# Gate rows moved from the head of the last projection into the stick-breaking stage, and the last reciprocal root moved from GpSimd to ScalarE

## The chip, the cores and the metric

The kernel runs on one core of a Trainium2 chip. That core has four engines that compute: TensorE (PE, its weight loads are listed apart as PEld), VectorE (DVE), ScalarE (ACT) and GpSimd (POOL). SyncE (SP) issues most of the transfers. Each engine works through its own queue in order and waits on semaphores for the others. The metric is the device time of one execution in microseconds (us), as the median of three runs.

## What is computed

Two layers of a streaming encoder on a sequence of 512 tokens, each of 1024 values in fp32, and a last RMS norm. The first layer has a pooling mixer and a spatial gate, the second a gated linear attention (GLA) and a stick-breaking attention of 8 heads. Each layer ends in an output projection of 2048 inputs on 1024 outputs, multiplied by a gate row and added to the residual stream. The reference, cut to what the change touches:

```python
def ada_modulate(x, c, norm_g, ada_w, ada_b):
    ada = jax.nn.silu(c) @ ada_w + ada_b
    shift, scale, gate = jnp.split(ada, 3, axis=-1)
    h = rmsnorm(x, norm_g) * (1.0 + scale[:, None, :]) + shift[:, None, :]
    return h, gate[:, None, :]
...
def odd_layer(x, c, norm_g, ada_w, ada_b, in_w, gate_w, gate_b, gla_norm_g, out_w):
    h, gate_res = ada_modulate(x, c, norm_g, ada_w, ada_b)
...
    y = jnp.concatenate([yc, yd], axis=-1) * jax.nn.silu(gate)
    return x + gate_res * (y @ out_w)
...
def rmsnorm(x, g):
    y = xf * lax.rsqrt(jnp.mean(xf * xf, axis=-1, keepdims=True) + EPS)
    return (y * g.astype(jnp.float32)).astype(x.dtype)
```

## The kernel before

**Matrix products.** Every fp32 operand is split into a high part of type fp32r and the remainder, also fp32r. ACT copies the high part (L183 for weights, L188 for activations), DVE subtracts (L184, L189), and TensorE runs three matmuls for each product (L197, L198, L199). One weight tile is 128x1024 fp32 (512 KB): SP loads it into one of 4 `raw` buffers (L166), and its split takes one of 3 `whi`/`wlo` pairs. One tile serves 24 matmuls of 128x512.

**Order.** A scheduler of the framework orders DVE, ACT, POOL and SP by readiness and program order. For the GLA and stick-breaking stages TensorE's order is written by hand: `boundary()` counts gaps of 12 matmuls, `at(g, f)` hangs a function on gap `g`, and `g0` is the first gap of the stick-breaking stage. Each head (`add_head`) adds score matmuls (L776), transposes (L803) and output matmuls (L811) between the projections' matmuls. The last two steps of GLA's second pair (`norm`, matmuls L719 and L720) still lie in the gaps behind `g0`. That stage ends at `order.close()`. PSUM has 6 banks with the tag `mm` for projections and 2 with the tag `aux` for everything else.

**Gate rows.** `gate_rows(1)` (L320, called at L878) makes the second layer's gate as rows that all partitions hold: eight times DVE multiplies a 128x128 tile of ones by one gate column (`rep`, L327), TensorE transposes it (L328), and for each four ACT copies the PSUM bank to `gbc` (L329). `rep` has 4 buffers (tag `diag`). The code stands behind the stick-breaking stage, and TensorE's order there is the scheduler's.

**Last projection.** `out_proj` (called at L896) runs outputs 0 to 511 for all four blocks of 128 tokens, 8 weight tiles of 24 matmuls; then outputs 512 to 1023 for blocks 0 and 1, and for blocks 2 and 3, 8 tiles of 12 matmuls each. After each block's last matmul DVE multiplies by `gbc` (L344) and adds to `x` (L345), and ACT squares with a sum over the row (L334). `scale_first` (L893) multiplies the first half of `x` by the norm's weights `fg`. `final` (L882) adds the two sums on DVE (`ssum`, L359), makes the reciprocal root on POOL in two 128x1 steps (L292, L293), scales the halves on ACT (L886) and DVE (L887), and sends them out through ACT's and SP's queues (L890).

Of the kernel before, what the change touches and what calls it, by code (L numbers as in the profile page):

```python
# [15 lines left out]
D = 1024  # L16
# [80 lines left out]
def trunk(ctx: ExitStack, tc: tile.TileContext, d, out):  # L97
# [8 lines left out]
    def nm(s):  # L106
        uid[0] += 1
        return f"{s}_{uid[0]}"
# [10 lines left out]
    def bank(tag="mm"):  # L119
        return psum.tile([P, 512], F32, name=nm(tag), tag=tag, bufs=MM_BUFS if tag == "mm" else 8 - MM_BUFS)  # L120
# [43 lines left out]
    def raw(src, w=1024):  # L164
        t = pool.tile([P, 1024], F32, name=nm("raw"), tag="raw", bufs=BUFS["raw"])
        nc.sync.dma_start(out=t[:, :w], in_=src)  # L166
        return t
# [12 lines left out]
    def split_w(t, w=1024):  # L180
        hi = pool.tile([P, 1024], F32R, name=nm("whi"), tag="whi", bufs=BUFS["w"])
        lo = pool.tile([P, 1024], F32R, name=nm("wlo"), tag="wlo", bufs=BUFS["w"])
        A.activation(out=hi[:, :w], in_=t[:, :w], func=AF.Copy)  # L183
        V.tensor_tensor(out=lo[:, :w], in0=t[:, :w], in1=hi.bitcast(F32)[:, :w], op=ALU.subtract)  # L184
        return hi, lo
# [21 lines left out]
    def stream(src, ahead=0):  # L207

        n, ready = [0], []

        def nxt():
            while len(ready) <= ahead and n[0] < src.shape[0]:
                ready.append(split_w(raw(src[n[0]])))
                n[0] += 1
            return ready.pop(0)

        def deepen(k):
            nonlocal ahead
            ahead = k
        nxt.deepen = deepen  # L220
        return nxt

    def c_unit(nxt, evac, between=lambda: None, quarter=lambda: None):
# [77 lines left out]
    def modulate(l, k, tbs, xn):  # L301
# [15 lines left out]
            V.tensor_copy(out=h_hi[k][:, r], in_=h[:, :w])  # L317
        V.tensor_tensor(out=h_lo[k][:, r], in0=h[:, :w], in1=h_hi[k].bitcast(F32)[:, r], op=ALU.subtract)  # L318

    def gate_rows(l):  # L320
        g = big("gbc")
        for n in range(2):
            ps = bank("aux")
            for i in range(4):
                c = 24 * l + 16 + 4 * n + i
                t = pool.tile([P, P], F32, name=nm("rep"), tag="diag", bufs=4)
                V.tensor_scalar(out=t, in0=ones, scalar1=ada[:, c:c + 1], scalar2=None, op0=ALU.mult)  # L327
                T.transpose(ps[:, i * P:(i + 1) * P], t, ident)  # L328
            A.copy(out=g[:, n * 512:(n + 1) * 512], in_=ps)  # L329
        return g  # L330


    def square(src, c):
        A.activation(out=junk, in_=src, func=AF.Square, accum_out=ss[:, c:c + 1])  # L334

    def out_proj(wo, y, gbc, ssc, after, mid=lambda: None):

        kept = {}

        def evac(n):  # L340
            def f(t, ps):
                c = slice(n * 512, (n + 1) * 512)
                u = slot("misc")
                V.tensor_tensor(out=u, in0=ps, in1=gbc[:, c], op=ALU.mult)  # L344
                V.tensor_tensor(out=x[t][:, c], in0=x[t][:, c], in1=u, op=ALU.add)  # L345
                square(x[t][:, c], ssc + 2 * t + n)
            return f
        t_unit(lambda kp: split_w(raw(wo[kp])), 8, y_left(y, range(TB), kept), evac(0))
        mid()
        late = lambda: None  # L350
        for tbs in ((0, 1), (2, 3)):
            t_unit(lambda kp: split_w(raw(wo[8 + kp])), 8, y_left(y, tbs, kept), evac(1), tbs,
                   ((tbs, (0, 1, 2)), late, (tbs, (3, 4)), (tbs[:1], (5, 6, 7)), (tbs[1:], (5, 6, 7))))
            late = after(tbs)
        return late
# [182 lines left out]

    def preload():
        pre.append(tc.keep_in_program_order(A.preload_act_table_set("natural_log_exp_and_others")))  # L540
    late = out_proj(d["wo0"], [y[i] for i in Y_ORDER[0]], gbc, 16, ln1, preload)


    nxt = stream(d["w1"])
# [63 lines left out]
    def at(g, f):  # L608
        steps.setdefault(g, []).append(f)
# [218 lines left out]
    def add_head(hd, g):  # L828
        block, wt = {}, {}
        at(g + 12, lambda: last.append(stick_out(hd, wt)))  # L830
        for i in range(3):
            at(g + i, lambda i=i: stick_weights(q[hd], k[hd], i, block))
            at(g + 9 + i, lambda i=i: stick_turn(block, TURNS[i], wt))
    g0 = gap[0]
    for c in range(4):
        add_head(2 * c, g0 + 12 * c + 8)
        add_head(2 * c + 1, g0 + 12 * c + 14)
# [14 lines left out]
    for c in range(4, 8):  # L852
# [7 lines left out]
        def evac(j, ps, sg=sg):  # L860
            held.append((sg, j, ps))
# [13 lines left out]
            held.clear()  # L875
    order.close()

    gbc = gate_rows(1)  # L878
    fg = big("fg")
    nc.sync.dma_start(out=fg, in_=d["fg"].to_broadcast([P, D]))  # L880

    def final(tbs):  # L882
        for t in tbs:
            r = token_rstd(t, 24)
            V.tensor_tensor(out=x[t][:, 512:], in0=x[t][:, 512:], in1=fg[:, 512:], op=ALU.mult)
            A.mul(out=x[t][:, :512], in_=x[t][:, :512], mul=r)  # L886
            V.tensor_scalar(out=x[t][:, 512:], in0=x[t][:, 512:], scalar1=r, scalar2=None, op0=ALU.mult)  # L887
            for n, e in ((1, nc.sync), (0, nc.scalar)):
                c = slice(n * 512, (n + 1) * 512)
                e.dma_start(out=out[t * P:(t + 1) * P, c], in_=x[t][:, c])  # L890
        return lambda: None

    def scale_first():  # L893
        for t in range(TB):
            V.tensor_tensor(out=x[t][:, :512], in0=x[t][:, :512], in1=fg[:, :512], op=ALU.mult)
    out_proj(d["wo1"], [y[i] for i in Y_ORDER[1]], gbc, 24, final, scale_first)  # L896


BUFS = {"big": 5, "y": 16, "kq": 8, "z": 6, "sp": 3, "r": 7, "misc": 3, "silu": 2, "raw": 4, "w": 3}
# [16 lines left out]
```

## Time and profile before

| | |
|---|---|
| Time, median of 3 runs | 843.73 us (843.17 to 845.31) |
| Profiled execution: time | 840.86 us |
| Profiled execution: span, first to last instruction | 839.0 us |
| PE busy | 817.4 us, 97% of the span |
| DVE, ACT, POOL busy | 61%, 47%, 7% |
| Mean granted TensorE clock | 0.997 |

The profile is of one execution. Starts are in microseconds from the span's first instruction. Matmuls are pipelined, so one that is listed with 0.39 us is followed by the next after some 0.23 us; what TensorE gets done is read from the starts. An idle time stands in brackets with the engine and line that ended it. Line numbers are those of the kernel before.

### The profile page before, as it was taken

The numbers are of one execution on the slowest core, as the hardware profiler recorded it, in microseconds if no ns is written. First come the engines' busy times: TensorE is split into PE (matmuls) and PEld (weight loads), VectorE is DVE, ScalarE is ACT, GpSimd is POOL, SyncE is SP. The second block draws the span as 40 slices with busy tenths as digits, with TensorE's granted clock in tenths as the row PEclk, the third lists the DMA queues.
The fourth block names the chain that finished last, engine by engine and source line by source line (L and its number), as shares of the span: only waits on it lengthen the run. The fifth ranks groups of instructions, "written<-read, shape, count | busy, mean of one in ns | idle before, by whom it ended". The sixth has DMA issues, their size and how long they took to land.

```text
span 839.0 us, 9962 instructions
## 1 busy us (share of the span) xinstructions
PE 817.4 (97%) x3688; PEld 660.5 (79%) x3688; DVE 512.2 (61%) x805; ACT 396.7 (47%) x663; POOL 61.0 (7%) x131
## 2 busy tenths in 40 slices
PE   5999999999999999999999999999999999989996
PEld 3878888888888887777878888877777777768884
DVE  6866664688684377743564543475757677433875
ACT  5463221233243356554353423575757678443553
POOL 3001111100000000000000000011010101020011
PEclk9999999999999999999999999999999999999998
DMA  8886555555562335412322221222221212222362
GB/s 285 307 290 208 189 157 195 182 169 166 187 200 79 101 126 177 161 67 100 101 76 65 78 84 51 93 84 75 76 76 53 88 39 98 78 98 97 113 206 87
DMA packets 31362, 108.31 MB, mean 129 GB/s; under 512 B 3633, under 2 KB 3761, under 8 KB 31314
## 3 DMA queue, kind: packets, MB, share of 16 engines
q1 hardware_dynamic: 30738, 106.63, 38.0%
q10 hardware_dynamic: 576, 1.05, 0.3%
q8 instruction: 29, 0.48, 0.2%
q14 instruction: 19, 0.16, 0.1%
HBM read 105.56 MB, written 2.10 MB: 128 GB/s over the span
## 4 chain that ended last, share of the span: by engine, by line
PE 89%; DVE 4%; DMA 3%; ACT 1%; issue 1%; POOL 1%; SPq 0%; POOLq 0%; ACTq 0%; DVEq 0%
PE mm L198 26%; PE mm L199 26%; PE mm L197 25%; PE aux L776 2%; PE aux L811 2%; DVE wlo L184 1%; DMA raw<-in_wfirst 1%; PE aux L803 1%; DVE raw L173 1%; DMA raw<-in_w 1%; PE aux L463 1%; PE aux L687 1%; DMA x<-in_x 1%; ACT whi L183 1%; PE aux L689 1%
## 5 line engine op out<-in xcount | busy, mean ns | idle before, releaser
L184 DVE TENSOR_TENSOR wlo<-raw,whi 128x1024 fp32r<-128x1024 f32 (+1 forms) x146 | 177.5, 1218 | 123.6 <-ACT whi L183 123.5
L183 ACT ACTIVATE whi<-raw 128x1024 fp32r<-128x1024 f32 (+1 forms) x146 | 152.5, 1044 | 197.7 <-PE mm L198 82.3
L197 PE MATMUL mm<-hhi,whi 128*128 128x512 f32 x576 | 233.3, 405 | 0.0
L199 PE MATMUL mm<-hhi,wlo 128*128 128x512 f32 x576 | 225.0, 391 | 0.0
L198 PE MATMUL mm<-hlo,whi 128*128 128x512 f32 x576 | 224.5, 390 | 0.0
L197 PEld LDWEIGHTS mm<-hhi,whi 128*128 128x128 f32 x576 | 108.2, 188 | 23.6 <-issue 2.7
L198 PEld LDWEIGHTS mm<-hlo,whi 128*128 128x128 f32 x576 | 108.3, 188 | 23.1 <-issue 1.9
L199 PEld LDWEIGHTS mm<-hhi,wlo 128*128 128x128 f32 x576 | 108.1, 188 | 23.3
L173 DVE CUSTOM_DVE_ANT_0 raw<-raw,sc,cols 128x1024 f32<-128x1024 f32 x48 | 61.5, 1283 | 53.7 <-DMA raw<-in_adaT 53.5
L197 PE MATMUL mm<-whi,hhi 128*128 128x512 f32 x192 | 78.2, 410 | 0.2 <-DVE hhi L317 0.2
L198 PE MATMUL mm<-wlo,hhi 128*128 128x512 f32 x192 | 76.2, 397 | 0.1
L199 PE MATMUL mm<-whi,hlo 128*128 128x512 f32 x192 | 74.6, 396 | 0.1
L199 PE MATMUL mm<-whi,r 128*128 128x512 f32 x160 | 62.6, 391 | 0.0
L197 PE MATMUL mm<-whi,r 128*128 128x512 f32 x160 | 62.4, 391 | 0.0
L198 PE MATMUL mm<-wlo,r 128*128 128x512 f32 x160 | 62.4, 390 | 0.0
L197 PEld LDWEIGHTS mm<-whi,hhi 128*128 128x128 f32 x192 | 36.4, 191 | 10.2 <-issue 2.1
L199 PEld LDWEIGHTS mm<-whi,hlo 128*128 128x128 f32 x192 | 36.5, 190 | 8.8 <-DVE hlo L318 1.0
L198 PEld LDWEIGHTS mm<-wlo,hhi 128*128 128x128 f32 x192 | 36.7, 191 | 7.5 <-DVE wlo L184 0.5
L188 ACT ACTIVATE r<-y 128x256 fp32r<-128x256 f32 (+1 forms) x60 | 27.0, 479 | 29.2 <-PE mm L199 23.2
L189 DVE TENSOR_TENSOR r<-y,r 128x256 fp32r<-128x256 f32 (+1 forms) x60 | 29.1, 509 | 19.1 <-PE mm L198 16.1
L198 PEld LDWEIGHTS mm<-wlo,r 128*128 128x128 f32 x160 | 30.0, 188 | 6.4 <-DVE wlo L184 0.3
L197 PEld LDWEIGHTS mm<-whi,r 128*128 128x128 f32 x160 | 30.0, 188 | 6.2
(185 smaller groups left out, 1028.3 us busy)
## 6 DMA issues: line engine op xcount, KB each, us to landing
raw<-in_w SPq DMA_DIRECT2D x90, 512.0 KB, 3.3
raw<-in_adaT SPq DMA_DIRECT2D x48, 512.0 KB, 4.0
raw<-in_wo SPq DMA_DIRECT2D x48, 512.0 KB, 3.3
raw<-in_wfirst SPq DMA_DIRECT2D x8, 384.0 KB, 4.4
x<-in_x SPq DMA_DIRECT2D x4, 512.0 KB, 5.2
kq<-in_poolw SPq DMA_DIRECT2D x4, 256.0 KB, 5.3
out<-x SPq DMA_DIRECT2D x4, 256.0 KB, 2.1
out<-x ACTq DMA_DIRECT2D x4, 256.0 KB, 2.6
```

What stands on the lines that cost most here:

```text
L173: V.tensor_tensor_reduce(out=t, in0=t, in1=sc, scale=1.0, scalar=cols[:, C_AB[l] + b:C_AB[l] + b + 1], op0=ALU.mult, op1=ALU.add, accum_ou ...
L183: A.activation(out=hi[:, :w], in_=t[:, :w], func=AF.Copy)
L184: V.tensor_tensor(out=lo[:, :w], in0=t[:, :w], in1=hi.bitcast(F32)[:, :w], op=ALU.subtract)
L188: A.activation(out=hi, in_=src, func=AF.Copy)
L189: V.tensor_tensor(out=lo, in0=src, in1=hi.bitcast(F32), op=ALU.subtract)
L197: T.matmul(o, lh, rh, start=start, stop=False)
L198: T.matmul(o, lh, rl, start=False, stop=False)
L199: T.matmul(o, ll, rh, start=False, stop=stop)
L463: T.matmul(ps[:, t * P:(t + 1) * P], v[t][:, hd * P:(hd + 1) * P], sguw[hd // 4][:, c], start=True, stop=True)
L687: T.matmul(ov, gv[c][p][:, c0:c0 + P], att[p][:, j * P:(j + 1) * P], start=True, stop=p == 0)
L776: T.matmul(ps[:, c0:c0 + (t + 1) * P], q[:, t * P:(t + 1) * P], k[:, :(t + 1) * P], start=True, stop=True)
L811: T.matmul(ps[:, s * P:], sv[hd // 4][s][:, hd % 4 * P:(hd % 4 + 1) * P], wt[s], start=s == 0, stop=s == 3)
```

## The change

`gate_rows` is cut into `gate_half`, which returns the transposes and the copy as a second step. Both halves of the second layer's gate are hung on gaps `g0 + 2` to `g0 + 5` of the hand-written order. The stream of the last projection's weights is made before the stage, and its first load and split stand at gap `g0 + 60` (`prime`). `final` no longer uses POOL: DVE prepares mean of the first half plus epsilon (`first_sum`, L905 of the changed kernel), and ACT takes `Ln` with the second half's sum and then `Exp` of minus one half of it. A load of the activation table that has both is written ahead of `scale_first`.

```diff
+        def prime():
+            ready.append(split_w(raw(src[n[0]])))
+            n[0] += 1
+        nxt.prime = prime
...
+    def gate_half(l, n):
+        reps = []
+        for i in range(4):
+            c = 24 * l + 16 + 4 * n + i
+            reps.append(pool.tile([P, P], F32, name=nm("rep"), tag="diag", bufs=4))
+            V.tensor_scalar(out=reps[i], in0=ones, scalar1=ada[:, c:c + 1], scalar2=None, op0=ALU.mult)
+        def turn(g):
+            ps = bank("aux")
+            for i in range(4):
+                T.transpose(ps[:, i * P:(i + 1) * P], reps[i], ident)
+            A.copy(out=g[:, n * 512:(n + 1) * 512], in_=ps)
+        return turn
...
-    def out_proj(wo, y, gbc, ssc, after, mid=lambda: None):
+    def out_proj(wo, y, gbc, ssc, after, mid, nxt):
...
-        t_unit(lambda kp: split_w(raw(wo[kp])), 8, y_left(y, range(TB), kept), evac(0))
+        t_unit(lambda kp: nxt(), 8, y_left(y, range(TB), kept), evac(0))
...
     g0 = gap[0]
+    gbc, turns = big("gbc"), []
+    wo1 = stream(d["wo1"])
+    at(g0 + 2, lambda: turns.append(gate_half(1, 0)))
+    at(g0 + 3, lambda: turns[0](gbc))
+    at(g0 + 3, lambda: turns.append(gate_half(1, 1)))
+    at(g0 + 5, lambda: turns[1](gbc))
+    at(g0 + 60, wo1.prime)
...
-    gbc = gate_rows(1)
...
+    def first_sum(t):
+        s = sm("msq")
+        V.tensor_scalar(out=s, in0=ss[:, 24 + 2 * t:25 + 2 * t], scalar1=1.0 / D, scalar2=EPS, op0=ALU.mult, op1=ALU.add)
+        return s
...
-            r = token_rstd(t, 24)
+            r = sm("rstd")
+            A.activation(out=r, in_=ss[:, 25 + 2 * t:26 + 2 * t], func=AF.Ln, scale=1.0 / D, bias=msq[t])
+            A.activation(out=r, in_=r, func=AF.Exp, scale=-0.5)
...
     def scale_first():
+        tc.keep_in_program_order(A.preload_act_table_set("natural_log_exp_and_others"))
         for t in range(TB):
+            msq[t] = first_sum(t)
             V.tensor_tensor(out=x[t][:, :512], in0=x[t][:, :512], in1=fg[:, :512], op=ALU.mult)
```

TensorE at the end of the stick-breaking stage, kernel before: the last matmuls of the stage's last projection (`mm_5753`), the eight transposes of the gate rows, and the first matmuls of the last projection (`mm_5871`).

```order
L199 MATMUL mm_5753<-hhi_125,wlo_5757 128x512
L328 MATMUL aux_5841<-ident,rep_5842 128x128
L328 MATMUL aux_5841<-ident,rep_5845 128x128
L328 MATMUL aux_5841<-ident,rep_5848 128x128
L328 MATMUL aux_5841<-ident,rep_5851 128x128
L197 MATMUL mm_5871<-whi_5877,kq_5881 128x512
L328 MATMUL aux_5855<-ident,rep_5856 128x128
L328 MATMUL aux_5855<-ident,rep_5859 128x128
L328 MATMUL aux_5855<-ident,rep_5862 128x128
L198 MATMUL mm_5871<-wlo_5878,kq_5881 128x512
L328 MATMUL aux_5855<-ident,rep_5865 128x128
L199 MATMUL mm_5871<-whi_5877,kq_5882 128x512
```

The same place in the changed kernel, where the last projection's bank is `mm_5877`:

```order
L198 MATMUL mm_5782<-hlo_133,whi_5785 128x512
L199 MATMUL mm_5782<-hhi_125,wlo_5786 128x512
L197 MATMUL mm_5877<-whi_5803,kq_5881 128x512
L198 MATMUL mm_5877<-wlo_5804,kq_5881 128x512
L199 MATMUL mm_5877<-whi_5803,kq_5882 128x512
L197 MATMUL mm_5877<-whi_5803,kq_5885 128x512
L198 MATMUL mm_5877<-wlo_5804,kq_5885 128x512
```

No transpose stands between the two projections any more, and the first product's three matmuls follow each other.

TensorE a few gaps behind `g0`, kernel before: the last matmul of a projection, the two matmuls of GLA's `norm`, and the next projection.

```order
L198 MATMUL mm_4109<-hlo_133,whi_4112 128x512
L199 MATMUL mm_4109<-hhi_125,wlo_4113 128x512
L719 MATMUL aux_4196<-r_4158,ones_r 128x512
L720 MATMUL aux_4196<-r_4159,ones_r 128x512
L197 MATMUL mm_4212<-hhi_118,whi_4164 128x512
L198 MATMUL mm_4212<-hlo_126,whi_4164 128x512
L199 MATMUL mm_4212<-hhi_118,wlo_4165 128x512
```

The same place in the changed kernel:

```order
L199 MATMUL mm_4110<-hhi_125,wlo_4114 128x512
L733 MATMUL aux_4205<-r_4159,ones_r 128x512
L734 MATMUL aux_4205<-r_4160,ones_r 128x512
L336 MATMUL aux_4221<-ident,rep_4181 128x128
L336 MATMUL aux_4221<-ident,rep_4183 128x128
L336 MATMUL aux_4221<-ident,rep_4185 128x128
L336 MATMUL aux_4221<-ident,rep_4187 128x128
L197 MATMUL mm_4235<-hhi_118,whi_4165 128x512
L198 MATMUL mm_4235<-hlo_126,whi_4165 128x512
L199 MATMUL mm_4235<-hhi_118,wlo_4166 128x512
```

Four of the transposes stand behind `norm`; the other four stand in the same way 24 matmuls later. On DVE the second half's four `rep` stand behind the last split of GLA's `norm` (L189), ahead of `y` (L726 before).

ACT at the end of the program, kernel before: blocks 2 and 3.

```order
L334 ACTIVATE junk,ss<-x_100 128x512
L886 ACTIVATE x_100<-x_100,rstd_6589 128x512
L890 DMA out<-x_100 128x512
L334 ACTIVATE junk,ss<-x_101 128x512
L886 ACTIVATE x_101<-x_101,rstd_6599 128x512
L890 DMA out<-x_101 128x512
```

The same in the changed kernel:

```order
L347 ACTIVATE junk,ss<-x_100 128x512
L911 ACTIVATE rstd_6592<-ss,msq_6202 128x1
L912 ACTIVATE rstd_6592<-rstd_6592 128x1
L914 ACTIVATE x_100<-x_100,rstd_6592 128x512
L918 DMA out<-x_100 128x512
L347 ACTIVATE junk,ss<-x_101 128x512
L911 ACTIVATE rstd_6600<-ss,msq_6205 128x1
L912 ACTIVATE rstd_6600<-rstd_6600 128x1
L914 ACTIVATE x_101<-x_101,rstd_6600 128x512
L918 DMA out<-x_101 128x512
```

Each block has two more 128x1 activations on ACT behind its square; POOL's eight instructions are gone. One ACT_TABLE_LOAD is added, behind the square of block 3's first half. Elsewhere, SP issues the load of `fg` 30 weight loads earlier (behind the wait for the same matmul, a state update of GLA's second pair), the `out` of block 1 ahead of the last weight load instead of behind it, and the load and split of the last projection's first weight tile stand where they stood, in SP's, ACT's and DVE's queues alike.

## Rows read from the trace of the kernel before

**Rows 1.** Busy time by stretch, columns: us, PE, PEld, DVE, ACT, POOL busy, clock, DMA.

```profile
530.00:545.00 15.00, 15.00 (x66) 12.09 (x65) 7.31 (x9) 6.68 (x10) 0.00 (x0) 1.00 0.25 85
560.00:735.00 175.00, 175.00 (x783) 137.26 (x782) 111.80 (x158) 116.50 (x203) 15.96 (x43) 1.00 0.23 78
735.00:744.00 9.00, 5.92 (x29) 4.26 (x28) 5.93 (x6) 5.83 (x10) 4.94 (x4) 1.00 0.20 80
```

**Rows 2.** Timeline, stage's end, PE and DVE: start, us, engine, line, operation, idle before.

```profile
738.22 0.39 PE L199 MATMUL mm<-hhi,wlo 128*128 128x512 f32 x1
738.45 0.60 PE L328 MATMUL aux<-ident,rep 128*128 128x128 f32 x4
...
743.42 1.21 DVE L184 TENSOR_TENSOR wlo<-raw,whi 128x1024 fp32r<-128x1024 f32 x1
...
743.95 0.40 PE L197 MATMUL mm<-whi,kq 128*128 128x512 f32 x1
```

**Rows 3.** PE's waits from 560 us to the end: us in total, times, longest.

```profile
PE aux L328 <- DVE rep L327: 3.1, 4, 0.9
```

**Rows 4.** Groups by line, 735 to 744 us: busy us, mean ns, idle before.

```profile
L858 POOL TENSOR_TENSOR y<-y,silu 128x512 f32<-128x512 f32 x4 | 4.9, 1264 | 26.6 <-ACT silu L378 26.6
L327 DVE TENSOR_SCALAR rep<-ones,ada 128x128 f32<-128x128 f32 x4 | 4.7, 1243 | 2.3 <-PE aux L328 2.3
...
L378 ACT ACT_TABLE_LOAD x1 | 1.3, 1283 | 0.0
```

**Rows 5.** All instructions on `rep`: duration ns min/median/max, first and last start.

```profile
L327 DVE TENSOR_SCALAR rep<-ones,ada x16: 272/278/1304, 67.6 to 742.2; 128x128 f32<-128x128 f32 x16
```

**Rows 6.** Chain that ended last, inside the stick-breaking stage: start, us, what.

```profile
704.60 0.44 PE aux L803 x4
```

**Rows 7.** Timeline of DVE near `g0`.

```profile
516.48 0.87 DVE L702 SCALAR_TENSOR_TENSOR st<-st,edec,aux 128x256 f32<-128x256 f32 x2 [0.34 <-PE aux L698]
```

**Rows 8.** Timeline, third (first two lines) and fifth weight tile for blocks 0 and 1.

```profile
790.49 1.22 DVE L184 TENSOR_TENSOR wlo<-raw,whi 128x1024 fp32r<-128x1024 f32 x1
...
792.50 0.39 PE L198 MATMUL mm<-wlo,z 128*128 128x512 f32 x1
...
792.48 1.06 ACT L183 ACTIVATE whi<-raw 128x1024 fp32r<-128x1024 f32 x1 [1.05 <-PE mm L199]
...
793.70 1.22 DVE L184 TENSOR_TENSOR wlo<-raw,whi 128x1024 fp32r<-128x1024 f32 x1
...
797.95 0.39 PE L198 MATMUL mm<-wlo,r 128*128 128x512 f32 x1
```

**Rows 9.** Timeline, second weight tile for blocks 2 and 3.

```profile
807.66 1.05 ACT L183 ACTIVATE whi<-raw 128x1024 fp32r<-128x1024 f32 x1
...
809.79 0.49 DVE L887 TENSOR_SCALAR x<-x,rstd 128x512 f32<-128x512 f32 x1
...
810.79 2.36 DVE L184 TENSOR_TENSOR wlo<-raw,whi 128x1024 fp32r<-128x1024 f32 x2
...
812.06 0.19 PEld L198 LDWEIGHTS mm<-wlo,kq 128*128 128x128 f32 x1 [0.56 <-DVE wlo L184]
```

**Rows 10.** Timeline of the end: last matmul, then ACT on block 3.

```profile
830.57 0.39 PE L199 MATMUL mm<-whi,r 128*128 128x512 f32 x1
...
832.98 0.19 ACT L334 ACTIVATION_READ_ACCUMULATOR junk<-x 128x1 f32 x1
...
834.67 0.72 ACT L886 ACTIVATE x<-x,rstd 128x512 f32<-128x512 f32 x1 [1.51 <-POOL rstd L293]
```

**Rows 11.** Timeline of ACT in the stick-breaking stage: `Exp` (L780), `Ln` (L781), two widths.

```profile
696.69 0.63 ACT L780 ACTIVATE sp<-sp 128x512 f32<-128x512 f32 x1
...
697.35 0.72 ACT L781 ACTIVATE sp<-sp,one_c 128x512 f32<-128x512 f32 x1
...
707.71 0.40 ACT L780 ACTIVATE sp<-sp 128x256 f32<-128x256 f32 x1
...
708.14 0.51 ACT L781 ACTIVATE sp<-sp,one_c 128x256 f32<-128x256 f32 x1
```

**Rows 12.** Timeline of SP: weight loads issued from 507 us on.

```profile
507.33 186.29 SPq L166 DMA_DIRECT2D raw<-in_w  x27
```

More of the change, by code (lines that the diff above doesn't have):

```diff
@@ L322, in gate_rows @@
         for n in range(2):
[L323 to L329, printed above, removed]
+            gate_half(l, n)(g)
         return g
@@ L540, in preload @@
         pre.append(tc.keep_in_program_order(A.preload_act_table_set("natural_log_exp_and_others")))
-    late = out_proj(d["wo0"], [y[i] for i in Y_ORDER[0]], gbc, 16, ln1, preload)
+    late = out_proj(d["wo0"], [y[i] for i in Y_ORDER[0]], gbc, 16, ln1, preload, stream(d["wo0"]))
     nxt = stream(d["w1"])
@@ L891, in final @@
         return lambda: None
+    msq = [None] * TB
     def scale_first():
+        tc.keep_in_program_order(A.preload_act_table_set("natural_log_exp_and_others"))
         for t in range(TB):
+            msq[t] = first_sum(t)
             V.tensor_tensor(out=x[t][:, :512], in0=x[t][:, :512], in1=fg[:, :512], op=ALU.mult)
-    out_proj(d["wo1"], [y[i] for i in Y_ORDER[1]], gbc, 24, final, scale_first)
+    out_proj(d["wo1"], [y[i] for i in Y_ORDER[1]], gbc, 24, final, scale_first, wo1)
 BUFS = {"big": 5, "y": 16, "kq": 8, "z": 6, "sp": 3, "r": 7, "misc": 3, "silu": 2, "raw": 4, "w": 3}
```

## The prediction

> **What bounds the kernel now.** TensorE does, with two gaps and a tail. I read the busy time by stretch first, then what PE waits for, then the timelines of the places. In the stick-breaking stage PE is busy for 175.00 of 175.00 us at clock 1.00, while DVE has 111.80 and ACT 116.50 [rows 1]: whatever is put on PE there lengthens the stage, and whatever is put on DVE or ACT does not unless PE comes to wait for it. Between 735 and 744 us PE is busy for 5.92 of 9 us [rows 1]. From 560 us on the list of PE's waits has one entry, the transposes of the gate rows waiting for the tiles that DVE makes for them [rows 3]. A second, short wait shows on the weight-load side only, at 812.06 us [rows 9]. After the last matmul, at 830.57 + 0.39 = 830.96 us, the program needs another 8.0 us to the span's end at 839.0 [rows 10].
>
> **Part 1, the gate rows leave the head of the last projection.** The last matmul of the stage starts at 738.22, and the next instruction 0.23 us later [rows 2]. I call 0.228 us a matmul's pace. With nothing in between, the last projection's first matmul would start at 738.45 and its fourth at 738.45 + 3 x 0.228 = 739.13. It starts at 743.95 [rows 2]. So 4.82 us go by there. Four transposes in a stream cost 0.44 us [rows 6], eight 0.88 us; the other 3.94 us are waits. The order makes the wait: the second four `rep` need the buffers of the first four, so DVE can begin only behind the first transposes. And they are slow: 1243 ns each there [rows 4] against a median of 278 ns over all sixteen [rows 5]. In the same stretch POOL runs four multiplies of 1264 ns [rows 4], nearly the same pace. The Trainium skill, GPSIMD Engine Reference, section 1. Specifications, says that GpSimd shares its SBUF interfaces with VectorE and that they collide with DVE instructions that have two SBUF inputs or use a two-port mode; these rows agree, and by it DVE's subtraction for the third weight tile, which takes the place of `rep` beside the same four multiplies, may be slowed as well.
>
> In the new place the 0.88 us of transposes are paid in full, as PE has no idle time there. The waits should not come back. The first four `rep` are made long before and their transposes wait for nothing. The other four can begin once those have run, and PE needs them 24 matmuls later, 24 x 0.228 = 5.47 us. Four at 278 ns are 1.1 us, and between 530 and 545 us POOL has 0.00 and DVE 7.31 of 15 us busy [rows 1]. ACT gets the two copies of `gbc` there, with 6.68 us of 15 busy [rows 1].
>
> What is late next at the projection's head? Its first two tiles are split in both orders before the stage ends. The third tile's low part starts at 743.42 in the trace behind the `rep` [rows 2]; in the changed kernel PE wants it 48 matmuls after 738.45 + 0.88, at 750.3. Even if it had to sit out POOL's multiplies, it would be ready near 743.4 + 0.9 + 1.2 = 745.5, 4.8 us before that. So this part saves 4.82 - 0.88 = **3.94 us**.
>
> **Part 2, the first weight tile's load and split.** `prime` is to bring them forward, but the orders of SP, ACT and DVE have them where they were. **0 us.** The one thing that moves on SP is the load of `fg`. It passes 30 weight loads and waits for the same matmul, which DVE has already followed up at 516.48 [rows 7], before those loads come up. 0 us.
>
> **Part 3, the reciprocal root on ACT.** In the tail every step of block 3 hangs on the one before. The square's sum is read at 832.98 + 0.19 = 833.17, and ACT's multiply with the root starts at 834.67 [rows 10]: 1.50 us for one DVE add, two POOL steps and the hand-overs. After the change `Ln` and `Exp` of 128x1 stand there on ACT itself. No 128x1 activation of that kind is in the trace. `Exp` takes 0.63 us at width 512 and 0.40 at 256, `Ln` with a bias tile 0.72 and 0.51 [rows 11]; taken on in a straight line to width 1 that is 0.17 and 0.30. With three hand-overs of 0.03 us, the gap from the end of one dependent activation to the next (696.69 + 0.63 to 697.35, [rows 11]), this gives 0.56 us and saves **0.94 us**. The dear end takes the 256-wide prices, 0.40 + 0.51 + 0.09 = 1.00, and saves 0.50. The cheap end takes twice the accumulator read of 0.19 [rows 10], 0.47 with the gaps, and saves 1.03. I keep the line: its two points come from these functions. Block 2's root comes earlier too, but block 3's first DVE step waits for the last matmul either way, so that saves nothing. Three of the four `first_sum` stand on DVE ahead of the third tile's low part for blocks 0 and 1, which ends at 790.49 + 1.22 = 791.71 and is taken at 792.50 [rows 8]. At the price of the accumulator read, the nearest 128x1 step, they are 0.57 us under a cover of 0.79: 0 us.
>
> **Part 4, the table load.** It takes 1.28 us on ACT [rows 4], once, behind the squares. ACT is idle for 1.05 us before the high part of the fifth tile at 792.48, so that copy moves by about 0.24 us. Its low part starts at 793.70, 1.22 us long, and PE takes it at 797.95 [rows 8]: 3.0 us of cover. 0 us. The Trainium skill, ScalarE: Activation LUTs, section What ACT_TABLE_LOAD costs, speaks against this: it counts a drain with the load, about 2.66 us for a switch, twice what the row shows. By it the copy would move by about 1.6 us and half the cover would go, still 0 us in the sum; I raise the chance of the last rival by one hundredth for it.
>
> **Part 5, the short wait at 812.06.** DVE's low part of the second tile for blocks 2 and 3 is queued behind block 0's multiply with the root, which starts at 809.79 on POOL's word; the split follows behind it, and PE's weight load waits 0.56 us [rows 9]. In the changed order ACT makes the root behind the high part that starts at 807.66 [rows 9], ends at 808.71, with one 256-wide copy between `Ln` and `Exp`: 808.71 + 0.30 + 0.40 + 0.17 + gaps, about 809.6 us. That saves **0.2 us**. With the 256-wide prices for `Ln` and `Exp` it is 810.1, a loss of 0.3; at best the wait goes whole, and since PE catches up part of it I count 0.4.
>
> **Sum.** 3.94 + 0.94 + 0.2 = 5.1 us. The profiled execution took 840.86 us with a span of 839.0; it becomes 835.8 with a span of 833.9. The median of the runs shown is 2.87 us above the profiled one; I take the same 5.1 us from it: 843.73 - 5.1 = **838.6 us**. The bounds of the parts give 3.94 + 1.03 + 0.4 = 5.4 and 3.94 + 0.5 - 0.3 = 4.1, so 838.3 to 839.6. Half the spread of the three runs is 1.07 us; for two medians I add 1.5 on each side: 836.8 to 841.1.
>
> **The rivals.** *The wait moves along with the rows.* The second four `rep` still queue behind the first four transposes. Were they as late there as now, PE would lose the same 3.94 us in the stage and only parts 3 and 5 would stay, 1.1 us: 842.6. For it: the 4 buffers are unchanged. Against it: POOL is silent there, DVE has idle time, and 5.47 us lie between the two sets of transposes, more than even four slow `rep` take (4 x 1.243 = 4.97).
>
> *The tail gains nothing.* If two dependent activations of 128x1 cost the 1.50 us of the old path, part 3 is 0 and part 5 is the loss of 0.3: 843.73 - 3.6 = 840.1. Against it: even the 256-wide prices make 1.00 us.
>
> *Slower: SP is blocked by `fg`.* SP works in order, and in its new place `fg` stands ahead of 24 loads of the stage. SP issues 27 in 186.29 us, one in 6.9 us [rows 12], and 4 buffers hold 27.6 us of work. If `fg` were held for longer than that behind SP's normal time, PE would wait for weights, one for one; the kernel becomes slower from 27.6 + 5.1 = 32.7 us of blocking on. Held for 35.2 us, it gives 846.2. Against it: the matmul that it waits for is over by 516.48 [rows 7]. The same end would come from a table load that uses up its cover and stalls PE for more than 5.1 us, which the rows leave even less room for.
>
> **How the numbers follow.** The forecast of 838.6 gets 0.83, the tail without gain (840.1) 0.06, the wait that moves along (842.6) 0.07, the slower case 0.04, of which 0.01 is for the dearer table load. A measurement of this kernel tells about 0.3%, 2.5 us, from no change: faster means below 841.2, slower above 846.3. The first two cases are faster, 0.89; the third is the same, and so is a hundredth of the last, 0.08; 0.03 is slower. The range of 836.8 to 841.1 holds the first two and leaves out the others and the edges of the noise.
>
> **What would show it.** Part 1: PE's waits from 560 us on no longer name the gate's transposes; from the stage's last matmul to the projection's fourth three paces go by, and PE is busy for all of that stretch; near `g0` the `rep` take about 0.28 us and PE does not wait. Part 2: the first tile's high part stands as far ahead of the projection as now. Part 3: from the end of the accumulator read to ACT's multiply 0.5 to 1.0 us instead of 1.50, and from the last matmul to the end about 7.1 us instead of 8.0. Part 4: the fifth tile's low part ends before PE asks for it. Part 5: PE's weight load waits 0.4 us or less at the second tile of blocks 2 and 3. The prediction is wrong if a wait of more than 1 us shows anywhere on PE behind `g0`, or if 128x1 activations cost more than 0.5 us each.

## The result and the profile after

The changed kernel took 836.69 us as the median of four runs; before, on the same chip, it was 843.87 us. The ratio is 0.9907 with an interval of 0.9884 to 0.9930. Two more measurements on other occasions gave 0.9924 (0.9899 to 0.9949) and 0.9926 (0.9903 to 0.9949). The gain is thus some 6.2 to 7.8 us, where 5.1 were forecast. 836.69 lies 0.11 us below the range.

One of the four, the profiled one, was disturbed on the chip (1450.36 us), so the ratio goes by the other three, whose median of 836.02 us lies 0.78 us below the range, and the trace of the changed kernel here is that of its second measurement, `a_after` (838.42 us, span 836.7). The first lines of its page, busy time by engine:

```profile
span 836.7 us, 9961 instructions
...
PE 816.7 (98%) x3688; PEld 660.5 (79%) x3688; DVE 508.9 (61%) x805; ACT 399.4 (48%) x672; POOL 56.8 (7%) x123
```

Busy time by stretch, the answer to [rows 1] (us, PE, PEld, DVE, ACT, POOL busy, clock, DMA). The second row is the stretch at the projection's head, where before PE was busy for 5.92 of 9 us:

```profile
563.00:738.00 175.00, 175.00 (x784) 137.40 (x783) 112.35 (x158) 116.67 (x202) 16.44 (x43) 1.00 0.24 76
738.50:747.50 9.00, 9.00 (x42) 7.46 (x41) 2.94 (x2) 5.84 (x9) 5.53 (x4) 1.00 0.15 47
```

The timeline of that head, the answer to [rows 2], with PE's last stage matmul and the projection's first four (start, us, engine, line, operation), and the third tile's split beside POOL's multiplies. From the stage's last matmul to the fourth of the projection it is four paces of 0.228 us and nothing else:

```profile
741.73 0.39 PE L199 MATMUL mm<-hhi,wlo 128*128 128x512 f32 x1
...
741.96 0.39 PE L197 MATMUL mm<-whi,kq 128*128 128x512 f32 x1
...
741.97 6.02 POOL L879 TENSOR_TENSOR y<-y,silu 128x512 f32<-128x512 f32 x4 [26.62 <-ACT silu L392]
...
742.64 0.39 PE L197 MATMUL mm<-whi,kq 128*128 128x512 f32 x1
...
743.36 2.25 DVE L184 TENSOR_TENSOR wlo<-raw,whi 128x1024 fp32r<-128x1024 f32 x1 [3.41 <-ACT whi L183]
```

The gate rows in their new place, from the timeline: PE's transposes, DVE's second four tiles, ACT's copy. The four transposes stand in one block, with no idle time in front:

```profile
532.01 0.60 PE L336 MATMUL aux<-ident,rep 128*128 128x128 f32 x4
...
532.93 0.87 DVE L331 TENSOR_SCALAR rep<-ones,ada 128x128 f32<-128x128 f32 x4
...
533.24 0.59 ACT L337 COPY gbc<-aux 128x512 f32<-128x512 f32 x1
```

All instructions on `rep`, the answer to [rows 5]. None of the 16 tiles takes more than 290 ns:

```profile
L331 DVE TENSOR_SCALAR rep<-ones,ada x16: 280/284/290, 67.6 to 533.5; 128x128 f32<-128x128 f32 x16
```

The list of PE's waits from 560 us on, which held [rows 3], is empty. Over the whole span its longest entries are these (us in total, times, longest). The fourth has nothing to do with the change, and will matter:

```profile
PE aux L154 <- ACT c_row L150: 3.5, 1, 3.5
PE aux L312 <- DVE n L303: 3.0, 5, 1.0
PE aux L312 <- ACT n L386: 2.2, 1, 2.2
PE mm L199 <- DVE wlo L184: 2.0, 1, 2.0
```

The timeline of the end, the answer to [rows 10]: the last matmul, the accumulator read, `Ln` (L911), `Exp` (L912), the two multiplies and the transfer's issue:

```profile
828.94 0.39 PE L199 MATMUL mm<-whi,r 128*128 128x512 f32 x1
...
831.35 0.19 ACT L347 ACTIVATION_READ_ACCUMULATOR junk<-x 128x1 f32 x1
831.57 0.29 ACT L911 ACTIVATE rstd<-ss,msq 128x1 f32<-128x1 f32 x1
...
831.89 0.20 ACT L912 ACTIVATE rstd<-rstd 128x1 f32<-128x1 f32 x1
832.13 0.72 ACT L914 ACTIVATE x<-x,rstd 128x512 f32<-128x512 f32 x1
832.37 0.49 DVE L915 TENSOR_SCALAR x<-x,rstd 128x512 f32<-128x512 f32 x1
832.88 0.37 ACTq L918 DMA_DIRECT2D out<-x  x1
```

And the table load with the fifth tile's split behind it and PE's first use of that low part, the answer to [rows 8], and the short wait of [rows 9]:

```profile
790.09 1.28 ACT L924 ACT_TABLE_LOAD   x1
...
791.38 1.06 ACT L183 ACTIVATE whi<-raw 128x1024 fp32r<-128x1024 f32 x1
...
792.48 1.23 DVE L184 TENSOR_TENSOR wlo<-raw,whi 128x1024 fp32r<-128x1024 f32 x1 [0.15 <-ACT whi L183]
...
796.58 0.39 PE L198 MATMUL mm<-wlo,r 128*128 128x512 f32 x1
...
810.42 0.19 PEld L198 LDWEIGHTS mm<-wlo,kq 128*128 128x128 f32 x1 [0.27 <-DVE wlo L184]
```

**Where the time went, stage by stage.** The table is worked out from the starts of the same matmuls in several traces, us. `d_before` is a second trace of the kernel before, `k_before_cols` is described below. "Head" runs from the stage's last matmul to the 49th of the projection.

| | before | d_before | k_before_cols | a_after | a2_after |
|---|---|---|---|---|---|
| start to first layer's output projection | 258.20 | 263.04 | 258.51 | 260.73 | 260.29 |
| to the stick-breaking stage's last matmul | 480.02 | 480.02 | 480.19 | 481.00 | 481.04 |
| head | 15.98 | 17.57 | 18.45 | 11.11 | 11.11 |
| to the last matmul | 76.37 | 76.37 | 76.38 | 76.10 | 76.12 |
| to the end | 8.39 | 8.40 | 8.41 | 7.76 | 7.83 |

From the trace that the prediction was read from, the change takes 15.98 - 11.11 = 4.87 us off the head, pays 0.98 in the stage, takes 0.27 off the rest of the projection and 0.63 off the tail: 4.8 us. That is close to the sum of 5.1. But the other two traces with the old head have one that is 1.6 or 2.5 us longer still.

### The profile page after: what moved, and what is told of

It is laid out like the page before. It is cut to its first block, busy times and chain, and to the rows that moved or that the text cites. A ratio compares the mean times of both kernels' runs of the same rounds, so it can differ in the third digit from the quotient of the medians.

```text
span 1448.6 us, 9961 instructions
## 1 busy us (share of the span) xinstructions
PE 1432.0 (99%) x3688; PEld 853.2 (59%) x3688; DVE 515.5 (36%) x805; ACT 407.8 (28%) x672; POOL 57.2 (4%) x123
## 4 chain that ended last, share of the span: by engine, by line
PE 98%; DMA 0%; DVE 0%; ACT 0%; POOL 0%; issue 0%; SPq 0%; ACTq 0%; DVEq 0%
PE mm L197 29%; PE mm L199 29%; PE mm L198 29%; PE aux L825 2%; PE aux L790 2%; PE aux L817 1%; PE aux L477 1%; PE aux L701 1%; PE aux L312 1%; PE aux L712 1%; PE aux L703 1%; PE aux L674 1%; DMA x<-in_x 0%; PE aux L595 0%; PE aux L197 0%; PE aux L199 0%
## 5 line engine op out<-in xcount | busy, mean ns | idle before, releaser
L197 PE MATMUL mm<-hhi,whi 128*128 128x512 f32 x576 | 364.3, 633 | 0.0
L199 PE MATMUL mm<-hhi,wlo 128*128 128x512 f32 x576 | 349.0, 606 | 0.0
L198 PE MATMUL mm<-hlo,whi 128*128 128x512 f32 x576 | 348.9, 606 | 0.0
L199 PEld LDWEIGHTS mm<-hhi,wlo 128*128 128x128 f32 x576 | 140.1, 243 | 95.2 <-issue 64.5
L198 PEld LDWEIGHTS mm<-hlo,whi 128*128 128x128 f32 x576 | 141.7, 246 | 92.2 <-issue 65.9
L197 PE MATMUL mm<-whi,hhi 128*128 128x512 f32 x192 | 120.3, 630 | 0.3 <-DVE hhi L322 0.3
L198 PE MATMUL mm<-wlo,hhi 128*128 128x512 f32 x192 | 117.5, 612 | 0.0
L199 PE MATMUL mm<-whi,hlo 128*128 128x512 f32 x192 | 115.5, 612 | 0.0
L197 PE MATMUL mm<-whi,r 128*128 128x512 f32 x160 | 92.9, 582 | 0.0
L199 PE MATMUL mm<-whi,r 128*128 128x512 f32 x160 | 92.5, 578 | 0.0
L189 DVE TENSOR_TENSOR r<-y,r 128x256 fp32r<-128x256 f32 (+1 forms) x60 | 29.2, 511 | 67.6 <-PE mm L198 59.8
L199 PEld LDWEIGHTS mm<-whi,r 128*128 128x128 f32 x160 | 35.1, 219 | 26.3 <-issue 15.3
L197 PEld LDWEIGHTS mm<-whi,r 128*128 128x128 f32 x160 | 34.7, 217 | 26.0 <-issue 14.8
```

Of the source, the lines that this page charges most:

```text
L189: V.tensor_tensor(out=lo, in0=src, in1=hi.bitcast(F32), op=ALU.subtract)
L197: T.matmul(o, lh, rh, start=start, stop=False)
L198: T.matmul(o, lh, rl, start=False, stop=False)
L199: T.matmul(o, ll, rh, start=False, stop=stop)
```

## The experiments

Times of one batch come from one chip. The kernel before took 844.87 us in the first batch (33 runs), 844.25 in the second (17) and 842.46 in the third (20), always as medians.

**First batch: is the sum too small, and in which part?** Theory A takes the sum of 5.1 us for right and the rest for scatter; theory B takes one of its terms for too small by some 2 us. Each part of the change alone, and both ends again. `a_after` is the changed kernel, `d_before` the kernel before.

> The changed kernel once more. Theory A (the sum of the prediction, 5.1 us, is right; the other 2 to 3 us of the first result are the distance between the profiled execution of the kernel before, 840.86 us, and its median, 843.87 us, which is scatter of the kernel before and not an effect of the change): a span of 833.5 to 834.5 us in the trace, 0.5 to 1.0 us from the accumulator read to ACT's last multiply, no wait of the gate's transposes, and against runs of the kernel before on the same chip 4.5 to 5.7 us. Theory B (one term of the sum is too small by 2 us): 7 us or more against the kernel before on the same chip, and a place in the trace that gained more than its term.

> The kernel before, against itself, for a second trace and for the scatter. Theory A: the span of this second trace differs from the 839.0 us of the first by 2 us or more, in a stage that the change does not touch (the first 60 us, where DMA is busy), while the stages behind 735 us keep their length within 0.3 us. Theory B: the span is again near 839 us and the scatter small, so that the missing 2 us have to come from the change.

`b_gate_only` is the changed kernel with the old root:

```diff
-            r = sm("rstd")
-            A.activation(out=r, in_=ss[:, 25 + 2 * t:26 + 2 * t], func=AF.Ln, scale=1.0 / D, bias=msq[t])
-            A.activation(out=r, in_=r, func=AF.Exp, scale=-0.5)
+            r = token_rstd(t, 24)
...
-        tc.keep_in_program_order(A.preload_act_table_set("natural_log_exp_and_others"))
...
-            msq[t] = first_sum(t)
```

> The gate rows and the first split moved as in the change; the reciprocal root stays on GpSimd as before, without the table load. Theory A: 3.9 us less than before (3.5 to 4.3). Theory B, if the gate rows are the term that is too small: 6 us or more less.

`c_tail_only` is the opposite: the kernel before with `Ln`, `Exp` and the table load in the tail, and the gate rows where they were.

> The kernel before with the reciprocal root as logarithm and exponential on ACT and the table load; the gate rows stay where they were. Theory A: 1.1 us less than before (0.5 to 1.5). Theory B, if the tail is the term that is too small: 3 us or more less. A rival within A, that 128x1 activations are dear: no difference.

Measured: `a_after` 838.72, `d_before` 843.54, `b_gate_only` 839.01, `c_tail_only` 842.69 us. The rows give 843.54 - 839.01 = 4.5 us, the root 0.85, both 4.8; against the 33 runs of before the same three are 5.9, 2.2 and 6.2. So the times settle nothing about 1.5 us, but the traces do. In `c_tail_only` the span after the last matmul is 7.8 us and the stretch ahead of it 76.08, in `b_gate_only` they are 8.4 and 76.36: the tail's edit owns the 0.6 and the 0.3. Theory A's span for `a_after`, 833.5 to 834.5 us, was missed: it is 836.7, with 2.5 us more than the first trace ahead of the first layer's output projection. And `d_before`, a trace of the same program as before, shows at the head what the first trace did not, where theory A had expected the stages behind 735 us to keep their length within 0.3 us. Its timeline, PE:

```profile
743.06 0.39 PE L199 MATMUL mm<-hhi,wlo 128*128 128x512 f32 x1
743.29 0.60 PE L328 MATMUL aux<-ident,rep 128*128 128x128 f32 x4
743.65 0.48 PE L197 MATMUL mm<-whi,kq 128*128 128x512 f32 x1
744.82 0.30 PE L328 MATMUL aux<-ident,rep 128*128 128x128 f32 x1 [0.69 <-DVE rep L327]
745.95 0.33 PE L328 MATMUL aux<-ident,rep 128*128 128x128 f32 x1 [0.83 <-DVE rep L327]
747.17 0.33 PE L328 MATMUL aux<-ident,rep 128*128 128x128 f32 x1 [0.89 <-DVE rep L327]
...
748.40 0.33 PE L328 MATMUL aux<-ident,rep 128*128 128x128 f32 x1 [0.66 <-DVE rep L327]
...
749.68 0.63 PE L197 MATMUL mm<-whi,kq 128*128 128x512 f32 x1
750.11 0.63 PE L198 MATMUL mm<-wlo,kq 128*128 128x512 f32 x1
750.53 0.63 PE L199 MATMUL mm<-whi,kq 128*128 128x512 f32 x1
```

And its busy time in two stretches of 3.3 us behind the waits, columns as above:

```profile
749.30:752.60 3.30, 3.30 (x9) 2.60 (x8) 0.18 (x1) 0.58 (x2) 0.00 (x0) 0.50 0.48 159
752.70:756.00 3.30, 3.30 (x16) 2.73 (x15) 0.00 (x0) 0.61 (x1) 0.00 (x0) 1.00 0.00 0
```

Behind the four waits the granted clock is 0.50 (1.2 of 2.4 GHz), matmuls start 0.43 us apart instead of 0.23, and nine are begun where the next stretch of the same length begins sixteen. That lengthens the head from 15.98 to 17.57 us. PE counts as fully busy there, so neither its busy share nor its list of waits tells of it. Theory C, formed here: the waits cost their length and, in some executions, such a stretch behind them. Theory L: only their length.

**Second batch: take the waits away, leave the transposes.** `e_rep8` is the kernel before with four more buffers:

```diff
-                t = pool.tile([P, P], F32, name=nm("rep"), tag="diag", bufs=4)
+                t = pool.tile([P, P], F32, name=nm("rep"), tag="rep1" if l and n else "diag", bufs=4)
```

> The kernel before, with four buffers of their own for the second half of the second layer's gate tiles (rep): these four are then written in the first layer, TensorE has nothing to wait for at the head of the last projection, but all eight transposes stay there. Theory L (the head costs its own length and no more): the four waits of 3.1 us in all go, so about -3.0 us against before. Theory C (length and clock: behind the stall the granted clock falls from 1.00 to 0.50 in some executions, and matmuls start 0.43 us apart instead of 0.23): the stretch at half clock behind the head goes too, so -4 to -5 us, and no record at 0.50 between 740 and 765 us. A third view, that the transposes themselves are what costs: no gain, within 0.5 us of before.

Measured: 838.40 us, ratio 0.9930 (0.9916 to 0.9944), -5.9 us, mean clock 0.998 in the trace. Its timeline at the head, PE:

```profile
739.87 0.39 PE L199 MATMUL mm<-hhi,wlo 128*128 128x512 f32 x1
740.10 1.03 PE L328 MATMUL aux<-ident,rep 128*128 128x128 f32 x8
740.89 0.48 PE L197 MATMUL mm<-whi,kq 128*128 128x512 f32 x1
741.20 0.40 PE L198 MATMUL mm<-wlo,kq 128*128 128x512 f32 x1
```

Eight transposes in a row take 0.8 us and the head is 12.00 us long, 3.98 less than in the first trace and 5.6 less than in `d_before`. The clock does not fall. The 5.9 us, 4.7 to 7.1 by the interval, are more than theory L's 3.0 and at or above theory C's 4 to 5. The traces say more: with the transposes left where they were, the head gains what the move gained (15.98 - 11.11 - 0.98 = 3.89). What the rows' new place is worth is the end of the wait.

`f_rep2` goes the other way: two buffers for the second gate's tiles.

```diff
-                t = pool.tile([P, P], F32, name=nm("rep"), tag="diag", bufs=4)
+                t = pool.tile([P, P], F32, name=nm("rep"), tag="rep1" if l else "diag", bufs=2 if l else 4)
```

> The kernel before, with two buffers instead of four for the second layer's gate tiles: six tiles come late instead of four, and the scheduler lays the waits between the first tile's matmuls. Theory L: at most two more waits of 0.8 us, so 0 to +1.6 us against before, at the mean clock of before. Theory C: the stall is longer, so the stretch at granted clock 0.50 behind it is there in this profile and in more of the executions, +2 to +4 us.

Measured: 843.49 us, ratio 0.9995 (0.9978 to 1.0013). The size that was expected of theory C did not come: the stall is no longer than before (four waits of 2.9 us in all, where six tiles were late), since the scheduler laid matmuls of the first tile between them. Its trace does show the clock at 0.50 for 3.4 us behind the four waits, in a head of 17.35 us. But by the mean clock such stretches are in fewer of its executions, not in more as theory C had it: 8 of 12 lie at 0.996 or below, of the kernel before in the same batch 16 of 17.

`g_mult_dve` takes the neighbour away that made the tiles slow:

```diff
-                G.tensor_tensor(out=t, in0=t, in1=sg[j], op=ALU.mult)
+                V.tensor_tensor(out=t, in0=t, in1=sg[j], op=ALU.mult)
```

> The kernel before, with the four multiplies of 128x512 (L858) on VectorE instead of GpSimd. Both theories: the gate tiles (rep) take about 0.28 us instead of 1.24, because nothing of GpSimd runs beside them; if they stay near 1.2 us, the price was not GpSimd's. Theory L: the four waits of 0.9 us shrink to under 0.2 each, -2.5 to -3 us against before; less where the two multiplies ahead of the tiles on VectorE (about 0.7 us each) hold them up, then -1 to -1.5. Theory C: the same and 1 to 2 us more, with no record at clock 0.50 behind the head.

Measured: 839.02 us, ratio 0.9931 (0.9916 to 0.9947), -5.2 us. All instructions on `rep`:

```profile
L327 DVE TENSOR_SCALAR rep<-ones,ada x16: 276/278/287, 68.0 to 744.2; 128x128 f32<-128x128 f32 x16
```

And the timeline of DVE at the head:

```profile
742.36 1.29 DVE L858 TENSOR_TENSOR y<-y,silu 128x512 f32<-128x512 f32 x2 [1.99 <-ACT silu L378]
...
743.57 0.86 DVE L327 TENSOR_SCALAR rep<-ones,ada 128x128 f32<-128x128 f32 x4
```

The four tiles take 0.86 us together instead of 4.7 [rows 4], though they stand behind two of the multiplies now; PE's list names no wait for them, the head is 12.31 us long, and the clock there stays at 1.00. So the price of a tile was POOL's doing. In the first trace each of the four slow tiles ends some 0.08 us behind the end of one of POOL's four multiplies, the first at 739.83 against 739.75 us. The gain of 5.2 us is above theory L's 2.5 to 3 and a little above theory C's 3.5 to 5.

**The first layer's wait.** Ahead of the first layer's output projection `d_before` lost 4.8 us against the first trace (263.04 against 258.20). Most of it, and a part of the scatter, lies at one place that the change does not touch:

```profile
210.21 0.79 PE L199 MATMUL mm<-hhi,wlo 128*128 128x512 f32 x1 [2.77 <-DVE wlo L184]
210.80 0.63 PE L197 MATMUL mm<-hhi,whi 128*128 128x512 f32 x1
211.23 0.63 PE L198 MATMUL mm<-hlo,whi 128*128 128x512 f32 x1
```

This is PE in `d_before`: a wait of 2.8 us, and matmuls 0.43 us apart behind it, as the granted clock is 0.50 for 3.4 us there. Three more traces show the same near 210 us, `c_tail_only`, `f_rep2` and `g_mult_dve`, with waits of 2.5 to 2.8 us. The last of them has no fall at the head, and its mean clock is 0.995 all the same. So a low mean clock by itself does not say which of the two places made it. The split stands on DVE behind a product with conditioning weights whose load is late. The first trace has no such wait, `a_after` one of 2.0. The order of all instructions up to there is the same in both kernels. `i_cols_late` is the changed kernel with these loads spread:

```diff
-    for b in range(16, 24):
-        fill.append(lambda b=b: ada_block(1, b))
...
-        fillers(2)
+        fillers(1)
...
+    for b in range(16, 24):
+        at(2 * b - 24, lambda b=b: ada_block(1, b))
```

> The changed kernel, with half as many loads of the conditioning weights in the first layer's pooling stage, and the eight blocks that give the second gate's columns moved to the gaps 8 to 22 of the GLA stage. It is aimed at the wait near 209 us (2.0 us in the changed kernel's trace, 2.8 in a second trace of before, none in the first) that the change does not touch. Theory L: the wait goes, -2.0 us against the changed kernel, so -6.5 to -8 against before. Theory C: executions that show a lower mean clock go too, so -2 to -3.5 against the changed kernel, and less scatter. Rival: a load in the GLA stage makes TensorE wait there, or the head-of-line wait only moves on: no gain or slower than the changed kernel.

Measured: 836.10 us, ratio 0.9898 (0.9886 to 0.9911), four runs from 835.35 to 836.35. The wait is gone from the list, the first layer's output projection starts at 258.14, and 0.47 us of it come back between there and the stick-breaking stage's last matmul (481.47 us instead of 481.00).

**Third batch: the change with that scatter taken out.** `k_before_cols` is the kernel before with the same edit, so it differs from `i2_cols_late` by the change alone.

> The kernel before, with the conditioning loads of the first layer spread as in i_cols_late and nothing else: the wait near 209 us should be gone, the head of the last projection is that of before (late gate tiles, four waits). Against before: -2.8 us for the wait of d_before's trace and -1.6 us for the 3.4 us at half clock behind it, where an execution has them; about -3 us by the median. What this run tells apart: if the fall of the clock behind the head needs only the head, it is there in this trace too (matmuls 0.43 us apart near 748 us); if it needs the earlier fall as well (in the traces so far the two come together), the records show none, as in the first trace of before.

> The changed kernel with the same spread loads, again, beside k_before_cols on one chip: the two differ by the change alone, and the scatter of the first layer is out of both. Theory L (the sum of the prediction, 3.94 + 0.94 + 0.2): i2_cols_late is 5.1 us faster than k_before_cols. Theory C (the head also costs 1.6 us at half clock in most executions): 6 to 6.7 us faster. If the sum itself was too small elsewhere: over 7 us.

> The changed kernel again, as the neighbour of the other three on this chip. Theory L: 5.1 us faster than before; theory C: 6 to 7 us; i2_cols_late 2 to 3 us faster than this one, h_no_prime the same.

Measured: `k_before_cols` 841.17 us, ratio 0.9979 (0.9962 to 0.9997); `i2_cols_late` 837.19, 0.9932 (0.9910 to 0.9954); `a2_after` 835.94, 0.9926 (0.9903 to 0.9949). `k_before_cols` gained 1.3 us on the kernel before, where some 3 were expected. Its busy time by stretch, from its third wait on and then behind that:

```profile
742.60:749.30 6.70, 6.16 (x15) 4.59 (x16) 2.52 (x3) 1.11 (x2) 1.31 (x2) 0.50 0.22 78
749.50:753.00 3.50, 3.50 (x17) 2.90 (x16) 0.00 (x0) 1.06 (x1) 0.00 (x0) 1.00 0.00 0
```

And PE's timeline there:

```profile
747.74 0.63 PE L198 MATMUL mm<-wlo,kq 128*128 128x512 f32 x1
748.16 0.63 PE L199 MATMUL mm<-whi,kq 128*128 128x512 f32 x1
```

So the clock falls at the head with no fall in the first layer: 6.8 us at 0.50, from the third wait on, and a head of 18.45 us. In the traces of the two kernels the change is 18.45 - 11.11 = 7.3 us at the head, of which 1.3 come back ahead of it (481.50 against 480.19), and 0.3 and 0.6 at the end: 6.9 us. The medians differ by only 4.0 us, at six and twelve runs that spread over 3.3 and 3.7 us; resampling these runs gives 2.8 to 5.6 us. That is less than either theory said and holds theory L's 5.1, not theory C's 6 to 6.7: the pair that was to tell the two apart by their times does not bear out theory C's price. Nor is `i2_cols_late` faster than `a2_after`, though `i_cols_late` was the fastest of all. Whether the spread loads beat the changed kernel is not settled.

`h_no_prime` is the changed kernel without the line `at(g0 + 60, wo1.prime)`.

> The changed kernel without the early first load and split of the last projection (prime). By the prediction this part is worth 0: the same time as the changed kernel within 0.7 us. Rival: the first tile's split now comes behind other work of VectorE and TensorE waits for it at the head, +0.5 to +1.3 us (one split on ScalarE and VectorE).

Measured: 837.02 us (835.23 to 841.88), ratio 0.9940 (0.9919 to 0.9960). The median is 1.1 us above `a2_after`, inside the spread of either; by that number alone it could be the rival's 0.5 to 1.3. But the rival's wait at the head is not in the trace, which has the same stages as the changed kernel's: 481.00, a head of 11.11, then 76.08 us.

## Why the prediction was right and wrong

**Part 1, right in mechanism and size.** 3.94 us were forecast; the head and the stage give 4.87 - 0.98 = 3.89. The waits did not come back: the `rep` took 0.28 us, PE was busy for 9.00 of 9.00 us. The third tile's low part, foreseen 4.8 us ahead of its use, ended at 743.36 + 2.25 = 745.61, 7.2 us ahead of the 49th matmul at 752.84. It was slowed beside POOL's multiplies from 1.21 us [rows 2] to 2.25, hidden. One sign was miscounted: the three paces from the stage's last matmul to the projection's fourth are four by the prediction's own sum (738.22 to 739.13), and four were measured.

**Part 2, right by the traces.** The one without `prime` has the same stages, and no wait for `fg` shows.

**Part 3, right in mechanism, too large by half.** The tail gained 0.63 us, forecast 0.94. The gap from accumulator read to multiply fell from 1.50 us [rows 10] to 832.13 - 831.54 = 0.59, forecast 0.56. But from the last matmul to the end 8.0 became 7.4, not 7.1. Before, SP's transfer went off at 835.15 and ACT's at 835.43. Now DVE takes up its multiply 0.24 us behind ACT's, because its multiply with `fg` ends only then, and both transfers are issued at 832.88. They land later. Issues from 828 us on, of before and then of `a_after` (KB each, median us to landing):

```profile
out<-x SPq DMA_DIRECT2D x2, 256.0 KB, 2.0
out<-x ACTq DMA_DIRECT2D x2, 256.0 KB, 2.5
```

```profile
out<-x SPq DMA_DIRECT2D x2, 256.0 KB, 2.6
out<-x ACTq DMA_DIRECT2D x2, 256.0 KB, 2.7
```

The 0.3 us missing are lost there. All six traces with the new tail have 2.5 or 2.6 us on SP's queue and 2.7 or 2.8 on ACT's, all seven with the old one 2.0 or 2.1 and 2.5. That the shared issue is why was not tried.

**Part 4, right.** The load took 1.28 us and ACT's next copy began 1.29 us after the load's start, so the copy moved by about 0.27 us; the low part was ready at 793.71 and wanted at 796.58, 2.9 us of cover against 3.0 foreseen. The Trainium skill, ScalarE: Activation LUTs, section What ACT_TABLE_LOAD costs, has 2.66 us with a drain; this trace does not agree, no drain shows in it.

**Part 5, right.** The wait at the weight load fell from 0.56 to 0.27 us, and the stretch to the last matmul from 76.37 to 76.10.

**The step that failed is the last one of the sum: "I take the same 5.1 us from it".** The median stood 2.87 us above the profiled execution, and I treated those 2.87 us as something that both kernels carry. In most executions a part of them was made by the very wait that the change removes. Of five traces of kernels with the late tiles, four (`d_before`, `c_tail_only`, `f_rep2`, `k_before_cols`) have the clock at 0.50 at the head for 3.4 or 6.8 us; the one without is the trace that I read. With the same order on TensorE, the head is 15.98 us long in that trace and 17.57, 18.35 and 18.45 in the others: a price of 1.6 to 2.5 us. Of the eight traces of kernels without the late tiles (`a_after`, `a2_after`, `b_gate_only`, `e_rep8`, `g_mult_dve`, `h_no_prime`, `i_cols_late`, `i2_cols_late`) none has it there. The mean clock of the timed executions agrees: of 82 of the kernel before only six have 0.997, as the first trace, and those took 839.7 to 843.0 us; the other 76 lie at 0.992 to 0.996. Of 19 of the changed kernel 16 lie at 0.997 to 0.999. The first layer's wait lowers this number too, so the cleanest count is that of the kernels whose traces no longer have that wait: 10 of 12 executions of `k_before_cols` lie at 0.994 to 0.996, all ten of `i_cols_late` and `i2_cols_late` at 0.997 or 0.998.

The traces and these counts show that the change ends a stretch at half clock in most executions. That this is all of what the forecast lacked is not shown. With 4.8 us in every execution and 1.6 to 2.5 more in most, some 6.4 to 7.3 us are to be expected, and 6.2 to 7.8 were measured; but without the first layer's wait in either kernel it was 4.0, and taking that wait out made the kernel before faster by 1.3 us and the changed kernel not at all (837.19 against 835.94). So a part of the surplus may be that wait, which the change does not touch, if by chance it was longer or more frequent in the runs of before.

The range missed for the same reason: it took the head's price at one end only, as if the matmuls behind the waits ran as fast as elsewhere.

**The rivals.** The wait did not move along with the rows, the tail did gain, and `fg` held nothing up; each is refuted by the rows above.

**What stays open.** How many of the missing 2 us are the clock's at the head, and how many the first layer's; why the first trace kept its clock with the same four waits; why two kernels that differ by 6.9 us in their traces differ by 4.0 us in their medians; and what decides how late the conditioning load near 198 us comes, with the same order of instructions each time.

## What to carry to other kernels

A wait on TensorE can cost more than its length, since the matmuls behind it may run at half clock while they count as busy; look at the granted clock behind each wait in more than one trace before pricing it. When the median stands above the profiled execution, ask which part of that surplus the change itself removes. And before work is moved to escape a wait, see whether a few buffers end it: 2 KB in each partition took as much off the head here as the move did.

## What the hardware showed that I had not expected

The granted clock fell from 1.00 to 0.50 at a chain of four waits of 0.3 to 0.9 us with transposes between them, in four of five traces, and stayed there for 3.4 or 6.8 us: in `d_before` and `f_rep2` behind the fourth wait, in `c_tail_only` and `k_before_cols` already in the third.

The two kinds of instruction on DVE that met POOL's four multiplies lost nearly the same, about 1 us each: a 128x128 multiply by a column went from 278 to 1243 ns, a 128x1024 subtraction from 1.21 to 2.25 us. Without the multiplies on POOL, in `g_mult_dve`, they took 278 ns and 1.22 us. POOL lost as well: its third multiply in `a_after`, beside that subtraction, took 2.28 us, the other three 1.28 to 1.30. The Trainium skill, GPSIMD Engine Reference, section 1. Specifications, names the shared SBUF interfaces, and these rows agree.
